# The second post-norm of a hybrid SSD / ConvFFN layer: five token tiles to ScalarE and GpSimd, three summed in PSUM, and one-column VectorE operations with scalar factors

## The chip, the cores and the metric

The kernel runs on one core of a Trainium2 chip. The core has five engines that each work through a queue of their own in order: TensorE (PE in the profile; its weight loads are PEld), VectorE (DVE), ScalarE (ACT), GpSimd (POOL) and SyncE (SP, which here issues the transfers to and from memory). SBUF is the on-chip memory of 128 partitions, PSUM the memory that TensorE's products are summed in. The metric is the device time of one execution in microseconds (us); lower is better.

## The reference, cut to what matters

One layer over 1024 latent tokens and 1024 features: a token mixer and a feed-forward network with a 3 x 3 convolution, each followed by a post-normalisation. All of it is float32. The part that the change touches is this:

```python
ALPHA = (2.0 * DEPTH) ** 0.25          # DEPTH = 1
EPS = 1e-6

def layer_norm(x):
    xf = x.astype(jnp.float32)
    mu = jnp.mean(xf, -1, keepdims=True)
    var = jnp.mean(jnp.square(xf - mu), -1, keepdims=True)
    return ((xf - mu) * lax.rsqrt(var + EPS)).astype(x.dtype)

def modulate(x, shift, scale):
    return layer_norm(x) * (1 + scale) + shift

def post_norm(x, y, gate, g, b):
    return layer_norm(ALPHA * x + gate * y) * g + b

x = post_norm(x, mix_lat, g1, ln1_g[l], ln1_b[l])                       # first post-norm
ffn_lat = conv_ffn(modulate(x, sh2, sc2), ffn_w_up[l], ffn_conv_w[l], ffn_conv_b[l], ffn_w_down[l], True)
x = post_norm(x, ffn_lat, g2, ln2_g[l], ln2_b[l])                       # second post-norm: the output
```

## The kernel before, in words

The tokens are held as eight tiles of 128 tokens (the partitions) by 1024 features, `xa[0]` to `xa[7]`. A float32 product is made of three products of parts (high by high, high by low, low by high). In the order of time the kernel has four stages that matter here.

- The mixer and its output projection (`out_tiles`), up to about 467 us.
- The first post-norm. `post1(t)` takes the statistics of a tile on VectorE (`ln_stats`, line 154), normalises it (lines 1063 and 1064), takes the statistics again for the FFN's own normalisation and applies that (`norm`); `post2` transposes two tiles on TensorE, scales them on ScalarE (line 188), rounds them on VectorE (line 193) and forms the low part on GpSimd (line 194). The tiles go from 7 down to 0, so the FFN's first products wait for tiles 1 and 0.
- The ConvFFN: for each of 44 channel tiles TensorE makes the up-projection, VectorE the convolution (line 1170, one source in PSUM, one in SBUF, one factor per partition), GpSimd the products and low parts, and TensorE the down-projection in pieces.
- The second post-norm (lines 1249 to 1323). Four channel tiles are left for the end: their products are summed in PSUM by token tile (`last_mm`, line 1266), for tiles 0 to 3 in parts ahead of time and for tiles 4 to 7 one after the other, 24 products each. `post_last(t)` then adds the sum to `xa[t]`, takes the statistics, normalises and sends the tile out.

In `post_last` the tiles are treated in two ways before the change. Tiles 1 and 3 have their statistics made by ScalarE (lines 1289 and 1294: a pass that sums and a pass that sums squares), the other six by VectorE (`bn_stats`, line 161). Tiles 0 to 3 are normalised by ScalarE (line 1299), and multiplied by `ln2_g` and shifted by `ln2_b` by GpSimd (lines 1300 and 1301, two passes of 128x1024 in SBUF); tiles 4 to 7 are normalised by VectorE in two passes (lines 1307 and 1308). The sums are added in place to `xa[t]` in SBUF, so every later VectorE pass reads SBUF alone.

The reciprocal deviation takes a handful of operations on one column, 128x1: `rstd` (line 147 and on) forms variance plus epsilon on VectorE, the square root on ScalarE (line 149), the reciprocal on VectorE (line 151), and `newton` (lines 137 to 141) a Newton step on VectorE: two products of two columns, one multiply-add with constants, one more product. `ln_stats` then forms minus the mean over the deviation (line 165). Both are also called with four or two columns earlier in the kernel; with one column only in the two post-norms.

PSUM is held as three tiles of two banks (`psa`) and two of one bank (`psb`). Tiles 2 and 6 of the second post-norm take two single banks each; the others take a pair. Tiles 5, 6 and 7 are the last users of theirs.

The kernel is written with a scheduler that orders each engine's instructions at build time by the order of the program and by its own estimate of when operands are ready, so operations of several token tiles stand interleaved in an engine's queue. That queue is then run strictly in order.

Of the kernel before, what the change touches and what calls it, by code (L numbers as in the profile page):

```python
# [26 lines left out]
def rev_ap(t, hi, n):  # L27
    """Free elements hi, hi-1, ... (n of them) of a two-dimensional tile or AP."""
    a = t[:, hi : hi + 1]
    return bass.AP(a.tensor, a.offset, [list(a.ap[0]), [-1, n]])  # L30
# [3 lines left out]
def hybrid_layer(  # L34
# [16 lines left out]
    def open_psum(na, nb):  # L51
        """PSUM as na tiles of two banks and nb of one."""
        if psx[0] is not None:
            psx[0].close()
        psx[:] = ExitStack(), na, nb
        psx.append(psx[0].enter_context(tc.tile_pool(name=f"ps{na}", bufs=1, space=PSUM, reuse_waits="tile")))
# [13 lines left out]
    # Memory that is handed from stage to stage: tags of [P, 1024] words.  # L70
# [11 lines left out]
    def half(tag, name, shape=(P, 512), dt=F32):  # L82
        """One of two tiles of 512 words of a tag of the small pool."""
# [27 lines left out]
    # columns: c 0:8, c_ctx 8:16, conv w 16:40 (tap*8+tile), conv b 40:48, norm_w 48:52, pool_scale 52:54,  # L111
    # b_ada of the first shift 54:62 and scale 62:70
# [21 lines left out]
    def newton(r, v, n, name):  # L134
        """One Newton step of r towards 1/sqrt(v)."""
        t = sm.tile([P, n], F32, tag=f"rt{n}", name=f"{name}_t")
        V.tensor_tensor(t, r, r, op=ALU.mult)
# [6 lines left out]
    def rstd(var, n, name, scale=1.0):  # L144
        """1/sqrt(var*scale + eps): square root, reciprocal, one Newton step."""
# [8 lines left out]
    def ln_stats(srcs, name):  # L154
        """Mean, 1/deviation and -mean/deviation of the rows of several token tiles, [P, tiles] each."""
# [9 lines left out]
        V.scalar_tensor_tensor(nmr, mv[:, :, 0], -1.0, r, op0=ALU.mult, op1=ALU.mult)  # L165
        return mv[:, :, 0], r, nmr

    def modulate(xns, c0, c1, sc, sh, hi, lo, tmps, lo_eng, name, via_act=False):
        """Transpose token tiles, scale and shift per feature, split into two parts; hi and lo are functions of a range
        of feature tiles."""  # L170
# [33 lines left out]
    def split(raw, hi, lo, eng=None):  # L204
        """hi = raw rounded to float32r, lo = raw - hi (exact)."""
# [3 lines left out]
    # ================= mixer =================  # L209
# [8 lines left out]
    def wblock(c0, name, tags=None):  # L218
        """128 columns of w_in in two parts."""
# [8 lines left out]
    def zload(j, q):  # L228
        """Half the rows of 264 columns: dt and z[0:248], or z[248:512]."""
# [17 lines left out]
    def load_wa(qd):  # L247
        """A quarter of the shift's and of the scale's columns."""
# [28 lines left out]
    hh = [htile("H0", "hh0"), htile("H1", "hh1")]  # L277
    hl = [htile("H2", "hl0"), htile("H3", "hl1")]
    ada1 = sl.tile([P, 2, 8, 2], F32, name="ada1")  # shift or scale, feature tile, latents or context

    def ada_quarter(qd):
        """Two feature tiles of the first shift and scale, for latents and context."""
# [35 lines left out]
    dtr = sl.tile([P, 10, 16], F32, tag="dtr", name="dtr")  # the 16: (group, direction, head of the group)  # L318
# [15 lines left out]
    def z_out(t, pt):  # L334
        """dt, and silu(z) of a token tile, kept in DRAM until the scan's outputs need it."""
# [90 lines left out]
    def proj_feat(w, pt, mids=()):  # L426
        """One 128-column block; the functions of mids are called between the feature tiles."""
# [51 lines left out]
    def dv(t, tl, d):  # L479
        """[P, 2 groups, 4 heads] of one direction."""  # L480
        return t[:, tl, :].rearrange("p (g d h) -> p g d h", g=2, d=2)[:, :, d, :]

    def decay_a(dct):
# [7 lines left out]
        # softplus(v) = max(v, 0) + log1p(exp(-|v|)); log1p(e) = 2 atanh(e / (2 + e))  # L491
# [896 lines left out]
```

## Time and profile before

| what | us |
|---|---|
| median of three executions | 1238.14 |
| lowest of them | 1237.48 |
| profiled execution, first to last instruction | 1238.0 |
| last product on TensorE begins | 1213.85 |
| last operation on VectorE ends | 1234.95 |
| busy in the profiled execution: TensorE / VectorE / GpSimd / ScalarE | 1159.4 / 988.0 / 467.0 / 375.3 |

The profiled execution's span stands 0.1 us beside the median. A row of the timeline gives the start, the duration, the engine, the line of the kernel, the operation, what is written and read, the shapes, and, in brackets, how long the engine was idle ahead of it and who ended that. A group "x2" is two instructions one behind the other. A row of busy time by stretch gives, for each stretch of the span, its length and then the busy time and instruction count of each engine, the granted TensorE clock, and the share and rate of the DMA engines. A row of the groups gives the busy time and the mean duration in nanoseconds, then the idle time ahead and its causes.

### The profile page before, as it was taken

The numbers are of one execution on the slowest core, as the hardware profiler recorded it, in microseconds if no ns is written. First come the engines' busy times: TensorE is split into PE (matmuls) and PEld (weight loads), VectorE is DVE, ScalarE is ACT, GpSimd is POOL, SyncE is SP. The second block draws the span as 40 slices with busy tenths as digits, with TensorE's granted clock in tenths as the row PEclk, the third lists the DMA queues.
The fourth block names the chain that finished last, engine by engine and source line by source line (L and its number), as shares of the span: only waits on it lengthen the run. The fifth ranks groups of instructions, "written<-read, shape, count | busy, mean of one in ns | idle before, by whom it ended". The sixth has DMA issues, their size and how long they took to land.

```text
span 1238.0 us, 14349 instructions
## 1 busy us (share of the span) xinstructions
PE 1159.4 (94%) x5463; PEld 943.4 (76%) x5463; DVE 988.0 (80%) x1426; ACT 375.3 (30%) x559; POOL 467.0 (38%) x243
## 2 busy tenths in 40 slices
PE   4999998889978998999999999999999999999992
PEld 2798877768756886788888888888888888888881
DVE  4788799999898889798777777777777777778958
ACT  2263566712344132432222212222212122222140
POOL 0010143353352033575353435353434344353254
PEclk9999998989889998999999999999999999999996
DMA  9848555556624011221110212110211112011012
GB/s 314 293 146 298 169 159 173 167 198 219 221 77 171 33 35 51 86 68 51 34 55 31 69 34 68 35 52 34 68 34 50 53 34 69 27 58 52 2 50 119
DMA packets 104637, 122.52 MB, mean 99 GB/s; under 512 B 7006, under 2 KB 83564, under 8 KB 104568
## 3 DMA queue, kind: packets, MB, share of 16 engines
q1 hardware_dynamic: 104567, 121.60, 30.3%
q8 instruction: 43, 0.70, 0.2%
q14 instruction: 27, 0.21, 0.1%
HBM read 106.82 MB, written 14.76 MB: 98 GB/s over the span
## 4 chain that ended last, share of the span: by engine, by line
PE 74%; DVE 16%; DMA 4%; issue 3%; ACT 1%; POOL 1%; SPq 0%; DVEq 0%; ACTq 0%; POOLq 0%
PE pu L1219 37%; PE pdn L1144 16%; PE pout L994 4%; PE px L433 4%; PE pz L332 4%; PE pl L1266 2%; DMA bc<-cs_scratch 1%; PE pu L1180 1%; DVE EU L631 1%; DMA wa<-in_w_ada_dram 1%; DVE pn_st L161 1%; DVE st L696 1%; PE pp L433 1%; DVE xa L1063 1%; PE pd L896 1%
## 5 line engine op out<-in xcount | busy, mean ns | idle before, releaser
L1170 DVE SCALAR_TENSOR_TENSOR cv<-pu,ffc,cv 128x945 f32<-128x945 f32 (+7 forms) x368 | 432.6, 1177 | 20.5 <-ACT cv L1162 10.7
L1219 PE MATMUL pu<-h2h,wul 128*128 128x512 f32 x656 | 205.5, 394 | 0.0
L1219 PE MATMUL pu<-h2h,wuh 128*128 128x512 f32 x656 | 205.2, 394 | 0.0
L1219 PE MATMUL pu<-h2l,wuh 128*128 128x512 f32 x656 | 204.5, 393 | 0.0
L1147 DVE TENSOR_TENSOR xa<-xa,pdn 128x512 f32<-128x512 f32 x128 | 87.4, 683 | 128.9 <-PE pdn L1144 128.6
L207 POOL TENSOR_TENSOR wul<-wur,wuh 128x1024 fp32r<-128x1024 f32 x44 | 106.0, 2409 | 207.9 <-ACT wuh L206 207.9
L1219 PEld LDWEIGHTS pu<-h2h,wuh 128*128 128x128 f32 x656 | 123.3, 188 | 28.9
L1219 PEld LDWEIGHTS pu<-h2l,wuh 128*128 128x128 f32 x656 | 123.3, 188 | 28.6
L1219 PEld LDWEIGHTS pu<-h2h,wul 128*128 128x128 f32 x656 | 123.3, 188 | 27.8
L206 ACT ACTIVATE wuh<-wur 128x1024 fp32r<-128x1024 f32 x44 | 46.3, 1054 | 237.1 <-PE pu L1219 221.5
L1144 PE MATMUL pdn<-wdh,gl 128*128 128x512 f32 x288 | 113.3, 394 | 0.0
L1144 PE MATMUL pdn<-wdl,gh 128*128 128x512 f32 x288 | 113.3, 393 | 0.0
L1144 PE MATMUL pdn<-wdh,gh 128*128 128x512 f32 x288 | 113.1, 393 | 0.0
L1242 POOL TENSOR_TENSOR wdr<-wdr,g2b 128x1024 f32<-128x1024 f32 x22 | 53.0, 2411 | 68.4 <-DMA wdr<-in_ffn_w_down_dram 68.4
L1238 POOL TENSOR_TENSOR cv<-cv,cv 128x1024 f32<-128x1024 f32 (+1 forms) x23 | 53.1, 2308 | 60.5 <-ACT cv L1237 60.4
L207 POOL TENSOR_TENSOR gl<-cv,gh 128x1024 fp32r<-128x1024 f32 (+1 forms) x23 | 53.4, 2320 | 42.3 <-ACT gh L206 42.3
L1144 PEld LDWEIGHTS pdn<-wdh,gh 128*128 128x128 f32 x288 | 54.1, 188 | 12.9
L1144 PEld LDWEIGHTS pdn<-wdh,gl 128*128 128x128 f32 x288 | 54.1, 188 | 12.4
L1144 PEld LDWEIGHTS pdn<-wdl,gh 128*128 128x128 f32 x288 | 54.1, 188 | 12.2
L1162 ACT ACTIVATE cv<-pu,ffc 128x1024 f32<-128x1024 f32 (+3 forms) x46 | 53.1, 1154 | 29.0 <-PE pu L1219 18.8
L1237 ACT ACTIVATE cv<-cv 128x1024 f32<-128x1024 f32 (+1 forms) x23 | 23.5, 1022 | 120.6 <-DVE cv L1170 120.6
L207 POOL TENSOR_TENSOR wdl<-wdr,wdh 128x1024 fp32r<-128x1024 f32 x22 | 52.8, 2414 | 4.7 <-ACT wdh L206 4.7
(348 smaller groups left out, 2142.9 us busy)
## 6 DMA issues: line engine op xcount, KB each, us to landing
wur<-in_ffn_w_up_dram SPq DMA_DIRECT2D x44, 512.0 KB
wad<-in_w_ada_dram SPq DMA_DIRECT2D x32, 512.0 KB
wdr<-in_ffn_w_down_dram SPq DMA_DIRECT2D x22, 512.0 KB
wa<-in_w_ada_dram SPq DMA_DIRECT2D x32, 256.0 KB
bc<-cs_scratch SPq DMA_DIRECT2D x32, 256.0 KB
xr<-in_x_dram SPq DMA_DIRECT2D x8, 512.0 KB
wx_r<-in_w_in_dram SPq DMA_DIRECT2D x8, 512.0 KB
m_scratch<-EU SPq DMA_DIRECT2D x16, 256.0 KB
```

Source lines behind the costliest of these rows:

```text
L206: S.activation(hi, raw, AF.Identity)
L207: (eng or G).tensor_tensor(lo, raw, hi.bitcast(F32), op=ALU.subtract)
L332: TE.matmul(pt[:, j * 512 : j * 512 + ZW], a, b[:, k % 4, :], start=first and i == 0, stop=last and i == 2)
L433: TE.matmul(pt[:, q * 512 : q * 512 + 512], a[:, k, :], b[q][:, k, :], start=k == 0 and i == 0, stop=k == KD - 1 and i == 2)
L994: TE.matmul(pt[:, nb * 512 : nb * 512 + 512], u, v[:, nb * 512 : nb * 512 + 512], start=first and i == 0, stop=last and i == 2)
L1144: TE.matmul(pt, u_, v_[:, s], start=i == 0, stop=i == n - 1)
L1147: V.tensor_tensor(xa[t][:, s], xa[t][:, s], pt, op=ALU.add)
L1162: S.activation(acc[:, a * 64 : b * 64], pt[:, a * 64 : b * 64], AF.Identity, bias=ffc[:, 396 + ct : 397 + ct], scale=ffc[:, 176 + ct : 177 ...
L1170: last = V.scalar_tensor_tensor(dst, pv[:, r0 + dy : r1 + dy, c0 + dx : c1 + dx], ffc[:, w * 44 + ct : w * 44 + ct + 1], dst, op0=ALU.mult ...
L1219: TE.matmul(pt[:, q * 512 : q * 512 + 512], a[:, k, :], b[q][:, k, :], start=k == 0 and j == 0, stop=k == KD - 1 and j == 2)
L1238: G.tensor_tensor(acc[:, s], acc[:, s], acc_v[:, s], op=ALU.mult)
L1242: G.tensor_tensor(raw, raw, g2b, op=ALU.mult)
```

## The change

Three things change; elsewhere the difference between the two files removes comments only.

1. With one column, `newton` uses three `tensor_scalar` operations in place of four operations. The factors that were second tensors are now per-partition scalars. `ln_stats` forms its third result in the same way. This holds for the sixteen calls in the first post-norm and, as far as `newton` goes, for the eight of the second.
2. In `post_last`, tiles 0 to 3 all take their statistics on ScalarE; tile 4 takes them on VectorE; tiles 0 to 4 are normalised by ScalarE and scaled and shifted by GpSimd.
3. Tiles 5, 6 and 7 have the residual added into PSUM: the sum stays there, the statistics are read from there, the first normalising pass is done in place there, and the second writes to SBUF. Tiles 6 and 7 go by halves, each half with a transfer of its own.

```diff
     def newton(r, v, n, name):
         t = sm.tile([P, n], F32, tag=f"rt{n}", name=f"{name}_t")
+        if n == 1:
+            V.tensor_scalar(t, r, r, v, op0=ALU.mult, op1=ALU.mult)
+            V.tensor_scalar(t, t, -0.5, 1.5, op0=ALU.mult, op1=ALU.add)
+            q = sm.tile([P, n], F32, tag=f"rq{n}", name=f"{name}_q")
+            V.tensor_scalar(q, t, r, None, op0=ALU.mult)
+            return q
         V.tensor_tensor(t, r, r, op=ALU.mult)
         V.tensor_tensor(t, t, v, op=ALU.mult)
...
     def ln_stats(srcs, name):
...
-        V.scalar_tensor_tensor(nmr, mv[:, :, 0], -1.0, r, op0=ALU.mult, op1=ALU.mult)
+        if n == 1:
+            V.tensor_scalar(nmr, mv[:, :, 0], r, -1.0, op0=ALU.mult, op1=ALU.mult)
+        else:
+            V.scalar_tensor_tensor(nmr, mv[:, :, 0], -1.0, r, op0=ALU.mult, op1=ALU.mult)
...
+    NPOOL = 5
+
     def post_last(t):
-        z = xa[t]
-        if accs[t][2] is not None and t < NT - 1:
-            V.tensor_tensor(z, z, accs[t][2], op=ALU.add)
+        z, pt = xa[t], accs[t][2]
+        late = t >= NPOOL
+        halves = [slice(nb * 512, nb * 512 + 512) for nb in range(2)]
+        dst = [accs[t][nb] if late else z[:, s] for nb, s in enumerate(halves)]
+        if pt is not None and t < NT - 1:
+            V.tensor_tensor(pt if late else z, z, pt, op=ALU.add)
         else:
+            for nb, s in enumerate(halves):
+                V.tensor_tensor(dst[nb], z[:, s], accs[t][nb], op=ALU.add)
+        if late or t == NPOOL - 1:
+            mv = sm.tile([P, 2], F32, tag="bmv1", name=f"pn2_{t}_mv")
+            st = sm.tile([P, 2, 6], F32, tag="bst", name=f"pn2_{t}_st")
             for nb in range(2):
-                s = slice(nb * 512, nb * 512 + 512)
-                V.tensor_tensor(z[:, s], z[:, s], accs[t][nb], op=ALU.add)
-        if t not in (1, 3):
-            mu, r, nmr = ln_stats([z], f"pn2_{t}")
+                V.bn_stats(st[:, nb, :], dst[nb])
+            V.bn_aggr(mv, st)
+            mu = mv[:, 0:1]
+            r = rstd(mv[:, 1:2], 1, f"pn2_{t}")
         else:
             sc = cvt(f"lnsc{t}")
             acc2 = sm.tile([P, 2], F32, tag="lnacc", name=f"lnacc{t}")
             S.activation(sc, z, AF.Identity, accum_out=acc2[:, 0:1])
             nmu = sm.tile([P, 1], F32, tag="nmu", name=f"nmu{t}")
-            mu = sm.tile([P, 1], F32, tag="mu", name=f"mu{t}")
             V.tensor_scalar(nmu, acc2[:, 0:1], -1.0 / D, None, op0=ALU.mult)
-            V.tensor_scalar(mu, acc2[:, 0:1], 1.0 / D, None, op0=ALU.mult)
             S.activation(sc, z, AF.Square, bias=nmu, accum_out=acc2[:, 1:2])
             r = rstd(acc2[:, 1:2], 1, f"pn2_{t}", scale=1.0 / D)
+        if not late:
             nmr = sm.tile([P, 1], F32, tag="nmr1", name=f"nmr{t}")
-            V.tensor_tensor(nmr, nmu, r, op=ALU.mult)
-        if t < 4:
+            if t == NPOOL - 1:
+                V.tensor_scalar(nmr, mu, r, -1.0, op0=ALU.mult, op1=ALU.mult)
+            else:
+                V.tensor_scalar(nmr, nmu, r, None, op0=ALU.mult)
             S.activation(z, z, AF.Identity, bias=nmr, scale=r)
             G.tensor_tensor(z, z, lng, op=ALU.mult)
             G.tensor_tensor(z, z, lnb, op=ALU.add)
             nc.sync.dma_start(out[0, t * P : (t + 1) * P, :], z)
+        elif t < NT - 1 and pt is not None:
+            V.scalar_tensor_tensor(pt, pt, mu, lng, op0=ALU.subtract, op1=ALU.mult)
+            V.scalar_tensor_tensor(z, pt, r, lnb, op0=ALU.mult, op1=ALU.add)
+            nc.sync.dma_start(out[0, t * P : (t + 1) * P, :], z)
         else:
-            n = 2 if t == NT - 1 else 1
-            for h in range(n):
-                s = slice(h * D // n, (h + 1) * D // n)
-                V.scalar_tensor_tensor(z[:, s], z[:, s], mu, lng[:, s], op0=ALU.subtract, op1=ALU.mult)
-                V.scalar_tensor_tensor(z[:, s], z[:, s], r, lnb[:, s], op0=ALU.mult, op1=ALU.add)
+            for nb, s in enumerate(halves):
+                V.scalar_tensor_tensor(dst[nb], dst[nb], mu, lng[:, s], op0=ALU.subtract, op1=ALU.mult)
+                V.scalar_tensor_tensor(z[:, s], dst[nb], r, lnb[:, s], op0=ALU.mult, op1=ALU.add)
                 nc.sync.dma_start(out[0, t * P : (t + 1) * P, s], z[:, s])
```

## The prediction

> **What bounds the kernel now.** I read the busy time by stretch first, then the timeline of the two stretches in which TensorE is not full, then the groups of the last stretch.
>
> ```profile
> span 1238.0 us, 14349 instructions
> ```
> ```profile
> core 0: us, PE busy (x) PEld busy (x) DVE busy (x) ACT busy (x) POOL busy (x), PEclk, DMA share, GB/s
> 440.00:480.00 40.00, 39.55 (x191) 32.02 (x189) 38.68 (x82) 15.19 (x28) 18.88 (x11) 1.00 0.23 66
> 480.00:498.20 18.20, 11.51 (x55) 8.90 (x55) 16.29 (x37) 6.57 (x15) 6.48 (x5) 0.81 0.00 0
> ...
> 1187.80:1214.30 26.50, 26.45 (x115) 21.11 (x113) 25.33 (x57) 11.30 (x18) 12.63 (x6) 1.00 0.10 40
> 1214.30:1238.00 23.70, 0.00 (x0) 0.00 (x0) 20.45 (x43) 0.61 (x3) 7.32 (x3) 0.56 0.34 133
> ```
> ```profile
> 700.00:900.00 200.00, 200.00 (x867) 162.61 (x866) 145.74 (x145) 44.29 (x42) 86.52 (x37) 1.00 0.16 48
> ```
>
> In the ConvFFN TensorE is busy 200 of 200 us, so whatever starts it earlier ends it earlier. It has two holes: 6.7 us (18.20 - 11.51) in the first post-norm, and the last 23.7 us, where it has nothing left and VectorE is busy for 20.45. Only these can give anything, and the change touches both. In the last stage VectorE is not slow by its work but by waits inside its instructions:
>
> ```profile
> 1198.01 2.41 POOL L1300 TENSOR_TENSOR xa<-xa,ln2g 128x1024 f32<-128x1024 f32 x1 [12.22 <-ACT xa L1299]
> ...
> 1209.86 2.40 POOL L1300 TENSOR_TENSOR xa<-xa,ln2g 128x1024 f32<-128x1024 f32 x1
> ...
> 1216.00 5.62 POOL L1301 TENSOR_TENSOR xa<-xa,ln2b 128x1024 f32<-128x1024 f32 x2
> ```
> ```profile
> 1187.87 1.22 DVE L1279 TENSOR_TENSOR xa<-xa,pl 128x1024 f32<-128x1024 f32 x1 [12.24 <-PE pl L1266]
> ...
> 1209.94 2.32 DVE L1297 TENSOR_TENSOR nmr<-nmu,pn_q 128x1 f32<-128x1 f32 x1
> ...
> 1221.25 0.14 DVE L147 TENSOR_SCALAR pn_v<-pn_mv 128x1 f32<-128x1 f32 x1
> ...
> 1227.83 0.68 DVE L1283 TENSOR_TENSOR xa<-xa,pl 128x512 f32<-128x512 f32 x1
> ...
> 1233.27 0.16 DVE L141 TENSOR_TENSOR pn_q<-pn_r,pn_t 128x1 f32<-128x1 f32 x1
> 1233.46 0.16 DVE L165 SCALAR_TENSOR_TENSOR pn_nmr<-pn_mv,pn_q 128x1 f32<-128x1 f32 x1
> 1233.54 1.41 DVE L1308 SCALAR_TENSOR_TENSOR xa<-xa,pn_q,ln2b 128x512 f32<-128x512 f32 x2
> ```
>
> At 1209.94 a product of two single columns takes 2.32 us and ends at 1212.26, with the GpSimd pass that runs beside it (1209.86 + 2.40). The same kind takes 0.16 at 1233.27, where GpSimd is done. A VectorE operation with two tensors in SBUF is held until the running GpSimd pass ends. The one-tensor operation at 1221.25 is not: 0.14 us, inside a GpSimd pass that ends at 1221.62. What the holds cost stands in the groups from 1187.8 on:
>
> ```profile
> L1308 DVE SCALAR_TENSOR_TENSOR xa<-xa,pn_q,ln2b 128x1024 f32<-128x1024 f32 (+1 forms) x5 | 7.4, 1499 | 0.0
> ...
> L137 DVE TENSOR_TENSOR pn_t<-pn_r 128x1 f32<-128x1 f32 x8 | 4.2, 537 | 0.0
> ...
> L141 DVE TENSOR_TENSOR pn_q<-pn_r,pn_t 128x1 f32<-128x1 f32 x8 | 3.3, 425 | 0.0
> L138 DVE TENSOR_TENSOR pn_t<-pn_t,pn_v 128x1 f32<-128x1 f32 x8 | 2.8, 364 | 0.0
> L165 DVE SCALAR_TENSOR_TENSOR pn_nmr<-pn_mv,pn_q 128x1 f32<-128x1 f32 x6 | 2.8, 464 | 0.1
> L1297 DVE TENSOR_TENSOR nmr<-nmu,pn_q 128x1 f32<-128x1 f32 x2 | 2.5, 1238 | 0.0
> ...
> L1299 ACT ACTIVATE xa<-xa,nmr,pn_q 128x1024 f32<-128x1024 f32 x2 | 2.5, 1237 | 6.3 <-DVE nmr L1297 6.3
> ...
> L1294 ACT ACTIVATE lnsc<-xa,nmu 128x1024 f32<-128x1024 f32 x2 | 2.3, 1138 | 0.0
> L1289 ACT ACTIVATE lnsc<-xa 128x1024 f32<-128x1024 f32 x2 | 2.1, 1062 | 9.0 <-DVE xa L1279 9.0
> ...
> L149 ACT ACT_TABLE_LOAD x1 | 1.3, 1283 | 0.0
> ```
>
> The five one-column groups take 15.6 us for 32 operations; at the unheld 0.16 us they would take 5.1. Line 1308 takes 7.4 for three whole passes and two halves; four times the 1.41 of its last row is 5.6. Holds: about 12.3 us.
>
> **The change part by part: the last stage.** Part 1 makes every one-column operation a one-tensor one. Part 3 gives every large VectorE pass one source in PSUM. That this combination, with a factor per partition, runs free beside GpSimd is shown by the convolution:
>
> ```profile
> 1172.55 2.43 POOL L207 TENSOR_TENSOR wdl<-wdr,wdh 128x1024 fp32r<-128x1024 f32 x1
> ```
> ```profile
> 1170.41 5.22 DVE L1170 SCALAR_TENSOR_TENSOR cv<-pu,ffc,cv 128x512 f32<-128x512 f32 x7
> ```
>
> Seven passes in 5.22 us, 0.75 each, through a GpSimd pass. So no VectorE operation of the new last stage should be held, and the end is the later of two chains.
>
> VectorE's chain. The last product begins at 1213.85 and takes 0.4. Tile 7's second addition begins at 1227.83 and the last pass ends at 1234.95, 7.1 us, of which 1.3 is a pass of tile 6 in between; with part of tile 6 still in the way I take 6.4: 1214.3 + 6.4 = 1220.7. From 1234.95 to the span's end it takes 3.05 us, so 1223.8. VectorE's other work hides under the products: it loses the statistics of tiles 0 and 2, tile 4's two passes and the holds, so there is no backlog at 1214.3. No row shows writing to PSUM from VectorE. Its bounds are 0.74 us a half pass (as line 1308's) and twice that; I take the first, being next to the convolution's 0.75 with a PSUM source. Twice would add some 2.6 us on tile 7's four such operations. A `tensor_scalar` with column factors lies between 0.14 (line 147) and 0.3, so at most 0.5 us on the last chain.
>
> GpSimd's chain. Ten passes instead of eight, 2.41 each: 24.1 us. Its start: the first addition ends at 1189.1; then on ScalarE the summing pass (1.06) and the squaring pass (1.14), with some 0.2 each to read out the sum, the table load and square root (some 1.5), five one-column operations at 0.19 each (from 1233.27 to 1233.46) with the hops between engines (some 0.7), and the normalisation (1.24). That is 1196.1 bare. If tile 1's two passes go in between it is 1198.7, if tile 2's go too 1201.3. I take 1198.0, where the first pass begins today and near the first two. So 1198.0 + 24.1 = 1222.1. A whole tile's transfer of 512 KB instead of 256 KB costs
>
> ```profile
> 1204.50:1205.00 0.50, 0.50 (x3) 0.40 (x3) 0.50 (x4) 0.50 (x2) 0.03 (x1) 1.00 1.00 410
> ```
>
> at 410 GB/s 0.6 us more than the 3.05 above, less what overlaps: 3.5. The end is 1225.6, behind VectorE's 1223.8. SP issues in order: if tile 4's transfer stands ahead of tile 7's, tile 7's two follow by about 1 us, inside the range. ScalarE's load (4 x 2.6 + 5 x 1.24 + 1.3 + square roots, some 20 us from 1189) runs faster than GpSimd's 4.8 a tile. **The last stage gives 1238.0 - 1225.6 = 12.4 us.**
>
> **The first post-norm.** Here VectorE sets when TensorE can go on:
>
> ```profile
> 448.73 1.07 DVE L137 TENSOR_TENSOR pn_t<-pn_r 128x1 f32<-128x1 f32 x1
> 449.83 1.21 DVE L138 TENSOR_TENSOR pn_t<-pn_t,pn_v 128x1 f32<-128x1 f32 x1
> ...
> 457.71 1.26 DVE L137 TENSOR_TENSOR ln_t<-ln_r 128x1 f32<-128x1 f32 x1
> ...
> 474.70 1.16 DVE L137 TENSOR_TENSOR ln_t<-ln_r 128x1 f32<-128x1 f32 x1
> ...
> 476.55 0.81 DVE L308 TENSOR_SCALAR xn<-xa,ln_mv,ln_q 128x1024 f32<-128x1024 f32 x1
> ...
> 489.94 1.35 DVE L308 TENSOR_SCALAR xn<-xa,ln_mv,ln_q 128x1024 f32<-128x1024 f32 x1 [0.57 <-PE h L177]
> ```
> ```profile
> 473.45 2.40 POOL L207 TENSOR_TENSOR wul<-wur,wuh 128x1024 fp32r<-128x1024 f32 x1 [4.43 <-ACT wuh L206]
> ...
> 489.45 1.29 POOL L194 TENSOR_TENSOR h2l<-h2t,h2h 128x512 fp32r<-128x512 f32 x1 [0.36 <-DVE h2h L193]
> ```
> ```profile
> 485.91 0.20 ACT L149 ACTIVATE ln_s<-ln_v 128x1 f32<-128x1 f32 x1 [4.98 <-DVE ln_v L147]
> ```
> ```profile
> 487.07 1.12 PE L177 MATMUL h<-mat,xn 128*128 128x128 f32 x4 [5.34 <-ACT h2t L188]
> ```
>
> TensorE's 5.34 us end with ScalarE's row at 485.91: a square root that stands in its queue ahead of the scaling and waits for VectorE. Four products are held there by 0.9, 1.1, 1.1 and 1.0 us, and seven calls on the way lose one operation each, 0.19 where it is dependent, less where it is interleaved: up to 1.3. Upper bound 5.4 us, under the 6.7 of the hole. Lower bound: the holds pass on whole to the next operation with two SBUF tensors, lines 1063 and 1064, which stay: 0, and a slip of the queues' order could cost a microsecond. I take 3.0, a little over half: the hold at 474.70 frees 0.7 at least, since line 308 would then wait for GpSimd until 475.85 instead of starting at 476.55. TensorE is full in the ConvFFN and VectorE is not (146 of 200 us), so the 3.0 go to the end whole.
>
> **Sum:** 1238.0 - 12.4 - 3.0 = 1222.6; the span stands 0.1 below the median, which I leave out.
>
> A rule that speaks against the change: the Trainium skill's SBUF — State Buffer, Who interferes with whom, says that `tensor_scalar` too can take the port pair that VectorE shares with GpSimd. VectorE: DVE Perf Modes, Mode 2×_2P, ties that to an outermost dimension that can be split evenly. The trace agrees for wide ones (line 308: 0.81 us free, 1.35 beside the GpSimd pass that ends at 490.74). The one-column row at 1221.25 was not held. By the rule at its widest the time would be that of the second rival.
>
> **The rivals.**
> - The first post-norm gives nothing: the holds move to lines 1063 and 1064. Then 1225.6, with 1223 to 1228 by the start of GpSimd.
> - The new one-column operations are held as the old ones were. Against it: 1221.25; for it: the rows have constants as factors, not columns. Then VectorE gets about one such operation through for each GpSimd pass and leaves the last pass, 1222.1 and some 1.5 for its turns, with the work that it now has from 1221.6 on, 13.3 us: 1236.9, and 3.05 to the end: 1240, slower than before. It decides against the change once VectorE has over 11.4 us of work left at GpSimd's end (1238.0 - 3.05 - 1223.6).
> - GpSimd, the new bound, starts late: each ScalarE pass pair queued ahead of the first normalisation adds 2.6 us. Three pairs put the start at 1203.9 and the end at 1228.5, or 1231.5 without the first post-norm's 3. It takes a start after 1213 to lose all, and nothing points there.
> - The whole hole of the first post-norm closes (6.7) and GpSimd starts at 1196.1: 1217 (1196.1 + 24.1 + 3.5 - 6.7), VectorE's chain giving the same floor (1223.8 - 6.7).
>
> **How the numbers follow.** The forecast 0.62 (1218 to 1226, its own range), no gain in the first post-norm 0.17, one-column operations held 0.07, a late GpSimd 0.08, the whole hole 0.06. The range 1217 to 1230 leaves out the held operations and half of the late starts, 0.11; its width is that of the start of GpSimd and of the first post-norm's 0 to 6.7. A measurement of this kernel tells about 2% from no change: 24.8 us. Faster than 1213.4 is under the floor of 1217 (0.02), slower than 1262.9 needs two rivals at once (0.01), within 2% is the rest (0.97).
>
> **What would show it.** Right: no one-column VectorE row over 0.3 us anywhere beside GpSimd; large passes of tiles 5 to 7 at 0.75 a half; ten GpSimd passes back to back from about 1195 on that timeline (3 earlier by the first part), the last one ending after VectorE's last; TensorE's wait at 487 shorter by 3. Wrong: one-column rows of 1 to 2.4 us; PSUM passes near 1.5 us a half; gaps between GpSimd's passes with ScalarE as the releaser; or VectorE's last row after GpSimd's.

## The result and the profile after

The changed kernel takes 1229.43 us in the median of four executions (1228.78 to 1230.26), the kernel before 1237.81 beside it: a ratio of 0.9932, with a 95% interval of 0.9918 to 0.9947. That is 8.4 us, inside the predicted range of 1217 to 1230 and inside 2%, but 6.8 us above the predicted 1222.6. One of the four executions of the kernel before took 1640.35 us; without it their median is 1237.48. The profiled execution has a span of 1227.9 us, 10.1 less than the one before.

Three rows of the timeline cut each execution into four stretches: the first up-projection product on TensorE, the first product of the ConvFFN's main loop, and the first addition of the last stage on VectorE. First those of the kernel before (its first addition, at 1187.87, is shown in the prediction), then those of the kernel after:

```profile
467.68 0.48 PE L1180 MATMUL pu<-h2h,wuh 128*128 128x512 f32 x1
...
514.50 0.62 PE L1219 MATMUL pu<-h2h,wuh 128*128 128x512 f32 x2
```
```profile
466.44 0.49 PE L1190 MATMUL pu<-h2h,wuh 128*128 128x512 f32 x1
...
511.30 0.62 PE L1229 MATMUL pu<-h2h,wuh 128*128 128x512 f32 x2
```
```profile
1185.33 1.22 DVE L1295 TENSOR_TENSOR xa<-xa,pl 128x1024 f32<-128x1024 f32 x1 [12.24 <-PE pl L1276]
```

| stretch | before | after | difference |
|---|---|---|---|
| mixer, up to the first up-projection product | 467.68 | 466.44 | -1.24 |
| first post-norm, up to the main loop's first product | 46.82 | 44.86 | -1.96 |
| ConvFFN, up to the first addition (1187.87; 1185.33) | 673.37 | 674.03 | +0.66 |
| last stage, up to the end (1238.0; 1227.9) | 50.1 | 42.6 | -7.6 |

The mixer's 1.24 us is no part of the change: in the twelve profiled executions of this study that product began between 462.2 and 469.3, in no order that goes with an edit. The other three stretches repeat closely, so the experiments below are read in them, and the medians beside them.

The last stage after, in the groups from 1185 on. Columns: what is done, busy time and mean duration in ns, idle time ahead:

```profile
L1322 POOL TENSOR_TENSOR xa<-xa,ln2g 128x1024 f32<-128x1024 f32 x5 | 11.9, 2388 | 13.0 <-ACT xa L1321 13.0
...
L1331 DVE SCALAR_TENSOR_TENSOR pl<-pl,pn_mv,ln2g 128x512 f32<-128x512 f32 x4 | 3.0, 750 | 0.0
L1332 DVE SCALAR_TENSOR_TENSOR xa<-pl,pn_q,ln2b 128x512 f32<-128x512 f32 x4 | 2.9, 744 | 0.1
...
L139 DVE TENSOR_SCALAR pn_t<-pn_r,pn_v 128x1 f32<-128x1 f32 x8 | 2.1, 267 | 0.1
L142 DVE TENSOR_SCALAR pn_q<-pn_t,pn_r 128x1 f32<-128x1 f32 x8 | 1.6, 207 | 0.0
```

In this stage nothing on VectorE is held any more: the one-column products, which had a mean of 364 to 537 ns (lines 137, 138 and 141), are now at 207 and 267, and the normalising passes at 0.74 to 0.75 a half, as lines with a PSUM source were in the convolution. GpSimd's passes run back to back. The end is in the timeline: GpSimd's first and last pass, VectorE's last pass, and SyncE's issues (SPq).

```profile
1196.28 2.42 POOL L1322 TENSOR_TENSOR xa<-xa,ln2g 128x1024 f32<-128x1024 f32 x1 [12.99 <-ACT xa L1321]
...
1218.01 2.35 POOL L1323 TENSOR_TENSOR xa<-xa,ln2b 128x1024 f32<-128x1024 f32 x1
```
```profile
1219.34 0.75 DVE L1332 SCALAR_TENSOR_TENSOR xa<-pl,pn_q,ln2b 128x512 f32<-128x512 f32 x1
```
```profile
1201.21 19.51 SPq L1324 DMA_DIRECT2D out_dram<-xa  x5
1220.81 0.38 SPq L1328 DMA_DIRECT2D out_dram<-xa  x1
1221.29 3.40 SPq L1333 DMA_DIRECT2D out_dram<-xa  x4
```

Line 1324 sends out tiles 0 to 4, lines 1328 and 1333 tiles 5 to 7. The fifth transfer of line 1324 waits for GpSimd's last pass, which ends at 1220.36 (1218.01 + 2.35), and the five transfers of tiles 5, 6 and 7 stand behind it in SyncE's queue. Tile 5 had been normalised by 1211.08 (1209.80 + 1.28), tile 6 by 1215.21 (1213.82 + 1.39):

```profile
1209.80 1.28 DVE L1327 SCALAR_TENSOR_TENSOR xa<-pl,pn_q,ln2b 128x1024 f32<-128x1024 f32 x1
...
1213.82 1.39 DVE L1332 SCALAR_TENSOR_TENSOR xa<-pl,pn_q,ln2b 128x512 f32<-128x512 f32 x2
```

The busy time by stretch (the last two columns are the DMA engines' share and rate) shows no transfer from 1220 to 1221 and then 2 MB at nearly full rate:

```profile
1220.00:1221.00 1.00, 0.00 (x0) 0.00 (x0) 0.09 (x1) 0.00 (x0) 0.36 (x1) 0.50 0.00 0
1221.00:1222.00 1.00, 0.00 (x0) 0.00 (x0) 0.00 (x0) 0.00 (x0) 0.00 (x0) 0.50 0.81 324
1222.00:1223.00 1.00, 0.00 (x0) 0.00 (x0) 0.00 (x0) 0.00 (x0) 0.00 (x0) 0.50 1.01 410
...
1226.00:1227.00 1.00, 0.00 (x0) 0.00 (x0) 0.00 (x0) 0.00 (x0) 0.00 (x0) 0.50 0.55 217
```

From the last pass to the end it is 7.5 us (1227.9 - 1220.36); before it was 3.05.

### The profile page after: what moved, and what is told of

The parts are those of the page before. It is cut to its first block, busy times and chain, and to the rows that moved or that the text cites. A ratio compares the mean times of both kernels' runs of the same rounds, so it can differ in the third digit from the quotient of the medians.

```text
span 1227.9 us, 14332 instructions
## 1 busy us (share of the span) xinstructions
PE 1158.6 (94%) x5463; PEld 940.4 (77%) x5463; DVE 968.0 (79%) x1393; ACT 380.3 (31%) x568; POOL 470.5 (38%) x245
## 4 chain that ended last, share of the span: by engine, by line
PE 72%; DVE 13%; issue 5%; DMA 4%; POOL 4%; ACT 1%; SPq 0%; POOLq 0%; DVEq 0%; ACTq 0%
PE pu L1229 37%; PE pdn L1154 16%; PE pout L1004 4%; PE pz L342 4%; PE px L443 3%; PE pu L1190 2%; DMA bc<-cs_scratch 1%; DVE EU L641 1%; POOL xa L1322 1%; DMA wa<-in_w_ada_dram 1%; POOL xa L1323 1%; PE pp L443 1%; PE pd L906 1%; DVE EU L620 1%; DVE st L706 1%
## 5 line engine op out<-in xcount | busy, mean ns | idle before, releaser
L1154 PEld LDWEIGHTS pdn<-wdh,gh 128*128 128x128 f32 x288 | 54.0, 188 | 12.4
```

Source lines behind the costliest of these rows:

```text
L1154: TE.matmul(pt, u_, v_[:, s], start=i == 0, stop=i == n - 1)
```

## The experiments

Profiled executions by stretch, as in the table above, and the times. The ratio is to the kernel before, run beside each.

| kernel | median us | ratio, interval | first post-norm | ConvFFN | last stage |
|---|---|---|---|---|---|
| before (profile above) | 1237.81 | 1 | 46.82 | 673.37 | 50.1 |
| after (profile above) | 1229.43 | 0.9932 [0.9918, 0.9947] | 44.86 | 674.03 | 42.6 |
| after, a second time | 1227.52 | 0.9921 [0.9901, 0.9941] | 43.70 | 674.03 | 42.6 |
| part 1 alone | 1230.96 | 0.9944 [0.9927, 0.9962] | 43.63 | 673.38 | 45.2 |
| all but part 1 | 1238.10 | 0.9993 [0.9979, 1.0008] | 46.72 | 674.03 | 48.6 |
| all but part 3 | 1233.05 | 0.9964 [0.9946, 0.9983] | 43.63 | 674.02 | 46.0 |
| old first post-norm | 1229.06 | 0.9940 [0.9919, 0.9960] | 46.82 | 674.03 | 42.6 |
| transfers of tiles 5 to 7 on ScalarE | 1224.85 | 0.9888 [0.9860, 0.9916] | 43.68 | 674.03 | 39.2 |
| four tiles on GpSimd | 1225.70 | 0.9896 [0.9877, 0.9914] | 44.84 | 674.03 | 38.4 |
| products ahead of the transposes | 1233.83 | 0.9961 [0.9946, 0.9976] | 46.90 | 675.64 | 42.6 |
| transfers on ScalarE, early table | 1223.25 | 0.9877 [0.9836, 0.9918] | 43.66 | 673.38 | 38.0 |
| the same, four tiles on GpSimd | 1224.04 | 0.9868 [0.9828, 0.9908] | 43.64 | 673.38 | 37.7 |

**Part 1 alone.** The kernel before with the one-column operations of the change.

```diff
+        if n == 1:
+            V.tensor_scalar(t, r, r, v, op0=ALU.mult, op1=ALU.mult)
...
-            V.tensor_tensor(nmr, nmu, r, op=ALU.mult)
+            V.tensor_scalar(nmr, nmu, r, None, op0=ALU.mult)
```

> The kernel before with part 1 of the change alone (one-column operations with scalar factors, in both post-norms); tiles, engines and PSUM as before. Theory A (a hold is taken by the next operation with two SBUF tensors): the one-column rows fall to 0.3 us or less, but lines 1063/1064 in the first post-norm and 1307/1308 in the second, which still read two SBUF tensors, become the ones that wait; the first post-norm gives 1.5 to 2 us, the last stage 1 to 5, so 1231 to 1235 against 1237.8 before. Rival B (the holds go away with the column products): the last stage gives all of the 10.5 us that the five column groups lost, 1226 or less. Rival C (tensor_scalar is held as well): 1237 to 1240.

The last stage went from 50.1 to 45.2. Its groups on VectorE:

```profile
L1316 DVE SCALAR_TENSOR_TENSOR xa<-xa,pn_mv,ln2g 128x1024 f32<-128x1024 f32 (+1 forms) x5 | 9.8, 1970 | 0.0
L1317 DVE SCALAR_TENSOR_TENSOR xa<-xa,pn_q,ln2b 128x1024 f32<-128x1024 f32 (+1 forms) x5 | 8.6, 1733 | 0.0
...
L138 DVE TENSOR_SCALAR pn_t<-pn_r,pn_v 128x1 f32<-128x1 f32 x8 | 2.0, 263 | 0.0
```

In the kernel before, the second of these two lines took 7.4 us (line 1308, in the prediction), and the first:

```profile
L1307 DVE SCALAR_TENSOR_TENSOR xa<-xa,pn_mv,ln2g 128x1024 f32<-128x1024 f32 (+1 forms) x5 | 5.4, 1085 | 0.0
```

Theory A: the one-column rows are free, 5.1 us in place of 15.6, but the two large passes, which kept two inputs in SBUF, take 18.4 us in place of 12.8, where free ones would take 11.2 (twice the prediction's 5.6). Of the 10.5 us that the small operations no longer take, 5.6 have moved to the next large ones, and 4.9 are gained.

**All but part 1.** The kernel after with the one-column operations of the kernel before (`if n == 0` in `newton` and `ln_stats`, and the old products in `post_last`).

> The kernel after without part 1: tiles, engines and PSUM as changed, but the one-column operations in their old form everywhere. Theory A (the scalar factors are what lets VectorE run beside GpSimd's ten passes, so parts 2 and 3 need part 1): every column product of the last stage is held to the end of a GpSimd pass, three for each of eight tiles; tile 7's three alone cost some 5 to 7 us, and the first post-norm loses its 2 us: 1234 to 1242. Theory B (VectorE has slack in the last stage under the transfers, so the holds there cost little): it loses only the first post-norm's 2 us and at most 1 more, 1231 to 1232.5.

Theory A: 48.6 us, so parts 2 and 3 without part 1 give 1.5, and part 1 is worth 6.0 on top of them. Not as the expectation had it, though: tile 7's own three products ran free at 0.16, after GpSimd's end. The loss lies earlier, in VectorE's chain: its last pass ends 45.7 us after the first addition in place of 34.8, and the end comes 2.9 behind it. Products of tiles 2 to 6 are held in it, two of them in these rows:

```profile
1202.78 2.26 DVE L148 TENSOR_TENSOR pn_q<-pn_r,pn_t 128x1 f32<-128x1 f32 x1
...
1219.63 2.05 DVE L144 TENSOR_TENSOR pn_t<-pn_r 128x1 f32<-128x1 f32 x1
...
1230.17 0.75 DVE L1332 SCALAR_TENSOR_TENSOR xa<-pl,pn_q,ln2b 128x512 f32<-128x512 f32 x1
```

The held products of tiles 2 and 3 also make ScalarE late with their normalisation, and so GpSimd itself, which now waits ahead of its fifth and its seventh pass and ends 3.9 us later; that is not what sets the end here:

```profile
1206.59 2.40 POOL L1322 TENSOR_TENSOR xa<-xa,ln2g 128x1024 f32<-128x1024 f32 x1 [1.57 <-ACT xa L1321]
...
1214.60 2.34 POOL L1322 TENSOR_TENSOR xa<-xa,ln2g 128x1024 f32<-128x1024 f32 x1 [3.14 <-ACT xa L1321]
```

**All but part 3.** The sums of tiles 5 to 7 go to SBUF again and both passes read SBUF alone; tile 4 stays on GpSimd.

```diff
-        dst = [accs[t][nb] if late else z[:, s] for nb, s in enumerate(halves)]
+        dst = [z[:, s] for s in halves]
...
-            V.tensor_tensor(pt if late else z, z, pt, op=ALU.add)
+            V.tensor_tensor(z, z, pt, op=ALU.add)
...
-            V.scalar_tensor_tensor(pt, pt, mu, lng, op0=ALU.subtract, op1=ALU.mult)
-            V.scalar_tensor_tensor(z, pt, r, lnb, op0=ALU.mult, op1=ALU.add)
+            V.scalar_tensor_tensor(z, z, mu, lng, op0=ALU.subtract, op1=ALU.mult)
+            V.scalar_tensor_tensor(z, z, r, lnb, op0=ALU.mult, op1=ALU.add)
```

> The changed kernel with the sums of tiles 5, 6 and 7 kept in SBUF as before (part 3 undone); parts 1 and 2 stay. Theory A (a large pass with two SBUF tensors is held by GpSimd, a pass with one tensor in PSUM is not): GpSimd is busy without a break from 1196 to 1220, so the ten pass rows of tiles 5 to 7 are held, rows of 2 to 3.5 us, GpSimd's own passes lengthen by the turns VectorE takes, and the end comes 4 to 9 us later than the changed kernel, 1233 to 1238. Rival B (only the one-column products were worth anything; the large passes fit between): within 1.5 us of the changed kernel, 1228 to 1231.

Its groups on VectorE, beside the 3.0 and 2.9 us of the kernel after, and GpSimd's multiplications, beside 11.9:

```profile
L1331 DVE SCALAR_TENSOR_TENSOR xa<-xa,pn_mv,ln2g 128x512 f32<-128x512 f32 x4 | 6.3, 1572 | 0.0
...
L1332 DVE SCALAR_TENSOR_TENSOR xa<-xa,pn_q,ln2b 128x512 f32<-128x512 f32 x4 | 4.9, 1262 | 0.0
...
L1327 DVE SCALAR_TENSOR_TENSOR xa<-xa,pn_q,ln2b 128x1024 f32<-128x1024 f32 x1 | 3.4, 3356 | 0.0
```
```profile
L1322 POOL TENSOR_TENSOR xa<-xa,ln2g 128x1024 f32<-128x1024 f32 x5 | 13.9, 2771 | 13.0 <-ACT xa L1321 13.0
```

Theory A, a little under its 4 to 9 us: the stage takes 46.0, and part 3 is worth 3.4 on top of the other two. The 3.4 came through GpSimd: without part 3 the two engines' large passes hold each other, and GpSimd's last pass ends 38.4 us after the first addition in place of 35.0, with the same 7.5 us from there to the end, since SyncE's queue waits for that pass here too. VectorE's last pass ends 41.8 after the first addition in place of 34.8, so part 3 shortened that chain by 7.0, of which the queue let 3.4 through. The queue is also why this kernel loses 0.8 against part 1 alone (45.2): VectorE's last pass ends 0.4 earlier than there (42.2), but the end is 4.2 behind it in place of 3.0.

**Transfers of tiles 5 to 7 on ScalarE.** The kernel after, with these five transfers issued from ScalarE's queue.

```diff
-            nc.sync.dma_start(out[0, t * P : (t + 1) * P, :], z)
+            nc.scalar.dma_start(out[0, t * P : (t + 1) * P, :], z)
...
-                nc.sync.dma_start(out[0, t * P : (t + 1) * P, s], z[:, s])
+                nc.scalar.dma_start(out[0, t * P : (t + 1) * P, s], z[:, s])
```

> The changed kernel with the transfers of tiles 5, 6 and 7 issued from ScalarE's queue instead of SP's. Theory A (SP's queue is in order, and tile 4's transfer, which waits for GpSimd's last pass at 1220.4, holds back the five transfers of tiles 5 to 7, 1.5 MB, so that 2 MB move after the last pass): tiles 5 and 6 leave earlier, only tile 4's and the end of tile 7's are left, and the end moves from 1227.9 to about 1224 in the profile, 3.5 to 4.5 us faster than the changed kernel: 1225 to 1226. Rival B (the end is GpSimd's last pass plus a fixed time for a transfer): within 1 us of the changed kernel, 1228.5 to 1230. Rival C (ScalarE's queue, now waiting with transfers, delays the square roots of tiles 6 and 7): 1230 or more.

The stage falls from 42.6 to 39.2. ScalarE's queue (ACTq) sends each tile out when it is done, while GpSimd's last pass still runs:

```profile
1208.78 0.37 ACTq L1328 DMA_DIRECT2D out_dram<-xa  x1
1212.25 1.00 ACTq L1333 DMA_DIRECT2D out_dram<-xa  x2
1214.01 0.20 ACT L156 ACTIVATE pn_s<-pn_v 128x1 f32<-128x1 f32 x1 [7.66 <-DVE pn_v L154]
1216.21 1.92 ACTq L1333 DMA_DIRECT2D out_dram<-xa  x2
```
```profile
1215.64 2.35 POOL L1323 TENSOR_TENSOR xa<-xa,ln2b 128x1024 f32<-128x1024 f32 x1
```

GpSimd's last pass ends at 1217.99, and the end at 1222.2 is 4.2 us later in place of 7.5. The two chains before it did not move: from the first addition it is 35.0 us to GpSimd's end and 34.8 to VectorE's, here and in the kernel after. That is theory A; rival C is out, since the square roots on ScalarE did not delay VectorE.

**Four tiles on GpSimd.** `NPOOL = 4` in place of 5: tile 4 is normalised in PSUM by VectorE, and its transfer too comes from line 1328.

> The changed kernel with four tiles on ScalarE and GpSimd instead of five (tile 4 is summed in PSUM and normalised by VectorE like tiles 5 to 7; tile 3 takes its statistics on VectorE). Theory A (GpSimd's tenth pass and the transfers queued behind it set the end): GpSimd ends 4.8 us earlier, at about 1215.6 on the profile of the changed kernel, the transfers of tiles 4 to 6 go out before VectorE's last pass, and the end is VectorE's last pass plus 3: VectorE gets some 2.5 us more to do, of which up to 2 reach its last pass (1220 to 1222): 1223 to 1225 on the profile, 3 to 5 us faster than the changed kernel, 1225 to 1227. Rival B (VectorE is the bound once it takes tile 4): its last pass moves by 2.5 to 4 us and the end with it, 1228 to 1231.

38.4 us, as theory A had it: GpSimd is done at 1215.32. Tiles 4 and 5, normalised by 1205.75 and 1210.54, wait for it in SyncE's queue behind tile 3's transfer, but they go out while VectorE finishes tile 7, and the end stands 3.6 behind VectorE's last pass (1219.81 + 0.75). That pass ends 34.8 us after the first addition, as in the kernel after, so tile 4's two passes did not reach it. The fifth tile on GpSimd, with SyncE's queue as it was, cost 4.2 us.

**The first post-norm, and the kernel after again.** Both in one series with the next experiment.

```diff
-        if n == 1:
+        if n == 1 and name.startswith("pn2"):
...
-        if n == 1:
+        if n == 0:
```

> The kernel after, with the first post-norm's one-column operations as they were before the change (the second post-norm's stay as changed). It measures the first post-norm's share alone. Theory A (the holds moved to the two large normalising passes, and a good half of TensorE's shorter wait was given back because the products right after it ran at half clock): slower than the kernel after by 1.3 to 2.2 us, 1230.7 to 1231.7; column products of 0.9 to 1.2 us again in the first post-norm, TensorE's wait there near 5.3 us, and a half-clock stretch of the same 6.5 us or so as with the shorter wait. Theory B (the predicted term of 3.0 was right and the shortfall lies in the last stage alone): slower by 3.0, 1232.4. Theory C (the first post-norm gave nothing): 1229.4.

> The kernel after, unchanged, beside the others of this series on the same chip: 1229.4, within 1 us. It is what the other runs of the series are set against.

The medians stand 1.5 apart with overlapping intervals, which settles nothing. The stretch does: 46.82 with the old operations, to the hundredth what the kernel before had, against 44.86 and 43.70 in the two profiles of the kernel after. The first post-norm's share is thus 1.96 us in one, as theory A had it, and 3.12 in the other, near theory B's 3.0; theory C is out. That the same kernel has two values is taken up at the end.

**Products ahead of the transposes.** TensorE's wait in the first post-norm (3.19 us after, 5.34 before) is at a transpose, with up-projection products ready behind it. Half of those are put ahead.

```diff
-        up_half(first[n], wu[n], 1)
-        if n == 1:
-            post2((3, 2), n32)
+        up_half(first[n], wu[n], 1, range(KD if n < 2 else 4))
+    post2((3, 2), n32)
+    up_half(first[2], wu[2], 1, range(4, KD))
```

> The kernel after, with half of the third channel tile's up-projection (twelve products, ready since 479) placed ahead of the transposes of tiles 3 and 2 in TensorE's queue and the other half behind them. Nothing else is changed. Theory A (TensorE's remaining wait in the first post-norm is an order of its queue, and the half clock follows from the idle time): no idle time over 1 us from 478 to 490 on the timeline, the granted clock stays at 1.00 there, and the gain is the 3.2 us of the wait and most of the half-clock loss of some 1.5 us: 1224.7 to 1226.2. Theory B (the clock falls at this place whatever TensorE does): idle gone, but products still at 0.43 us apart for some 6 us: about 1227. Theory C (the wait moves to the transposes of tiles 1 and 0, which wait for VectorE): a hole of 2 to 3 us near 487 to 492, and no gain over 1 us.

A miss: the median is 6.3 us above that of the kernel after in the same series. The wait is gone where it stood, shorter ones come at the next transposes, somewhat as theory C had it, and after the last of these products a third that none had:

```profile
483.67 0.66 PE L187 MATMUL h<-mat,xn 128*128 128x128 f32 x4 [1.46 <-ACT h2t L198]
485.30 1.12 PE L187 MATMUL h<-mat,xn 128*128 128x128 f32 x4 [0.98 <-ACT h2t L198]
...
509.11 1.11 PE L1229 MATMUL pu<-h2h,wuh 128*128 128x512 f32 x2 [3.91 <-DVE cv L1180]
```

The main loop needs the PSUM of the first channel tile, which VectorE's convolution gives back only then; its first step on ScalarE had come at 501.58, behind a rounding that waited for GpSimd. So the first post-norm took 46.90 us, and 1.6 more went in the ConvFFN. That wait is not TensorE's alone to close. The clock did not stay at 1.00 either, as theory A had wanted (rows at the end).

**Two further versions.** Both kernels move the transfers to ScalarE and load the square root's table while ScalarE is idle; the second also has `NPOOL = 4`.

```diff
+    warm = sm.tile([P, 1], F32, tag="warm", name="warm")
+    S.activation(warm, group[-1][1][:, T - 1 : T].bitcast(F32), AF.Sqrt, scale=0.0)
```

> The kernel after with two edits: the transfers of tiles 5 to 7 are issued by ScalarE, and a square root of one column is put behind ScalarE's last rounding of the last channel tile, so that the square root's table is loaded while ScalarE is idle. From the first addition of the last stage to the end, the kernel after takes 42.6 us and with the transfers alone moved 39.2. Theory A (in that second kernel VectorE's chain, 34.8 us from the first addition to its last pass, and GpSimd's, 35.0, end together, so that only the later of them counts): GpSimd starts and ends 1.3 us earlier, VectorE's last pass does not move, and the stage gives at most 0.3 more: 38.9 to 39.2 us. Theory B (GpSimd alone sets the end): the whole 1.3 us comes through, 37.9 us. The time lies between 1220 and 1226, by where the mixer ends.

> The same two edits with four tiles on GpSimd in place of five. GpSimd's chain loses two passes (4.8 us) and the two square roots' wait; VectorE takes tile 4's two passes from PSUM (2.6 us). Theory A (VectorE now sets the end alone, and its last pass stands 34.8 us behind the first addition whatever GpSimd does): the stage takes 38.2 to 38.6 us, as with four tiles and all transfers on SyncE (38.4), so the queue no longer matters. Theory B (tile 4's passes fall into VectorE's last chain): 40 to 41 us. Theory C (the early table also shortens VectorE's backlog): 37.5.

38.0 and 37.7 us. With five tiles GpSimd ends 33.7 us after the first addition (1.3 earlier, as theory A had it) and VectorE's last pass 34.6 after it, so VectorE sets the end; but the gain was theory B's, since the way from the later of the two to the end fell from 4.2 to 3.4, tile 4's transfer no longer coming last (SyncE had issued it by 1216.30, ScalarE the last of tile 7 by 1217.30). With four tiles VectorE's last pass did not move (34.8), and the result lies between theories A and C: ScalarE's queue still saved 0.7 against four tiles on SyncE, all of it behind VectorE's last pass. With the queue out of the way the fifth tile on GpSimd makes next to no difference (38.0 with it, 37.7 without); no run shows a gain from it. By the ratios both are 1.2% to 1.3% faster than before. Against the kernel after the intervals of the ratios touch or overlap, so that they beat it rests on the last stage, 4.6 and 4.8 us shorter.

## Why the prediction was right, and where it was not

**The sign and the range** held, and the mechanisms that carry the sum were there; their sizes were off. The point was 6.8 us too low. In the profiled execution 5.3 of them are found: the last stage gave 4.84 less than predicted, the first post-norm 1.04 less, the ConvFFN took 0.66 more, and the mixer, by chance, 1.24 less. The other 1.5 are the step from that span to the median time. The prediction set the span of the kernel before beside a median of other executions and found 0.1 between them; in the kernel after, one and the same execution has a span of 1227.9 and a time of 1229.71. Set against the prediction's own terms:

**The last stage: 12.4 predicted, 7.6 measured.** The prediction's 1225.6 is 37.73 us after the first addition; it took 42.57. GpSimd's start was 0.82 later (10.95 us after the first addition, 10.13 taken), its ten passes took 24.08 (24.1 taken), and the way from there to the end 7.54 (3.5 taken). 0.82 - 0.02 + 4.04 is the 4.84 that is missing.

**The step that failed** is the sentence on SyncE: "if tile 4's transfer stands ahead of tile 7's, tile 7's two follow by about 1 us, inside the range". The order was foreseen as a possibility, but it was priced at tile 7's two transfers alone and left out of the sum. Not only those but all five of tiles 5 to 7 stood behind, 1.5 MB that had been ready or nearly so; with tile 4's that is 2 MB, which at the 410 GB/s quoted for that step are some 5.1 us. With the 2.4 that are left of the 3.05 before when its last 256 KB are taken off (0.64), an estimate from these rows is 7.5, as measured. Moving those five to another queue gave 3.4 us back, and having no such wait (four tiles) 4.2. The Trainium skill (DMA: Bandwidth & Descriptors, Issuing engines are not separate DMA queues) says that issuing from several engines only saves the time that a sequencer takes to initiate a transfer. The measured 3.4 us are of another kind: the DMA engines stood idle from 1220 to 1221 and were then busy at 0.81 to 1.01 up to 1226, so it was not the issuing that cost, but the queue's wait for GpSimd with finished transfers behind it.

**No held operation** was right, and so was the rate of passes in PSUM: in the two post-norms no one-column row beside GpSimd over 0.27 us, and in the last stage 0.74 to 0.75 a half pass, at the lower of the two bounds. The rule of the Trainium skill that was weighed there (SBUF — State Buffer, Who interferes with whom) did not apply to one column. That parts 1 and 3 were each needed is shown by the runs without them: 6.0 and 3.4 us. Part 2's fifth tile was not needed: with four tiles the last stage is shorter (38.4 us against 42.6, and 37.7 against 38.0).

**VectorE's chain** was mis-sized without effect in the kernel after. Its last pass was to end 6.4 us after the products; it ended at 1220.09 (1219.34 + 0.75), 8.4 us after the last product's end (1211.31 + 0.40):

```profile
1211.31 0.40 PE L1276 MATMUL pl<-wdh,gl 128*128 128x512 f32 x1
...
1211.74 0.70 DVE L1298 TENSOR_TENSOR pl<-xa,pl 128x512 f32<-128x512 f32 x1 [0.48 <-PE pl L1276]
...
1212.47 0.69 DVE L1298 TENSOR_TENSOR pl<-xa,pl 128x512 f32<-128x512 f32 x1
```

The 6.4 were counted from tile 7's second addition, as the 7.1 before were, less a part of tile 6. But the first addition waits for the last product too and comes ahead of it (0.73 from start to start), and tile 6 stood in the way whole: from the second addition to the end of the last pass it took 7.62. So GpSimd, which the prediction had ending 1.4 us after VectorE, ended only 0.27 after it (1220.36): that GpSimd came last, as forecast, was near to luck. The chain shows once GpSimd is out of the way: in the kernels with four tiles it sets the end.

**The first post-norm: 3.0 predicted, 1.96 measured**, and 3.1 to 3.2 in six of the eight profiled executions that have this first post-norm and nothing else moved in it; in the other two 1.96 and 1.98. The mechanism was as described, but little of the holds moved: line 1073 has three held passes (2.21, 2.08 and 2.48 us where a free one takes 1.28), as its counterpart, line 1063, had before (2.23, 2.33 and 2.57), and only one held pass of line 1074 is new (2.20). TensorE's wait fell by 2.15, from 5.34 to 3.19, not by the 3 that the prediction gave as its sign. The 3.0 was a choice between bounds of 0 and 5.4, so that six executions come within 0.2 of it is in part luck; what parts the other two from them is a matter that the prediction did not have, TensorE's clock (below).

**"The 3.0 go to the end whole"** was nearly right: the ConvFFN took 0.66 us more in the kernel after. It takes 673.37 or 673.38 in the kernel before, with part 1 alone and in the two further versions, and 674.02 or 674.03 in the others but one (675.64, products ahead). So the step goes with the kernel and is not jitter; what makes it was not found, and the count of products is the same.

**The rivals.** No gain in the first post-norm, held one-column operations and a GpSimd late by whole pairs of passes are each ruled out by rows above; the whole hole closed in no run.

## What to carry to other kernels

When work moves from one engine to another, its transfer moves in the issuing queue too: list that queue in order, and for each entry that waits add up the bytes that are ready behind it. When an engine that holds another through a shared resource gets more work, free all of the other's operations, small and large; freeing only one kind moves the holds to the next. And where run-to-run jitter elsewhere is as large as the effect, compare stretches between two rows of the trace rather than spans.

## What the runs showed of the hardware

**The half clock comes in whole windows.** A stretch at half clock began during each long wait of TensorE in the first post-norm. Busy time by stretch; the granted clock is the third column from the end, and a value between 0.50 and 1.00 gives the moment of the step. The kernel before, after, and after with the transfers moved:

```profile
483.00:484.00 1.00, 0.00 (x0) 0.00 (x0) 1.00 (x1) 0.00 (x0) 0.00 (x0) 0.70 0.00 0
...
490.00:491.00 1.00, 1.00 (x5) 0.76 (x5) 1.00 (x1) 0.98 (x3) 0.74 (x1) 0.89 0.00 0
```
```profile
481.00:482.00 1.00, 0.00 (x0) 0.00 (x0) 0.60 (x4) 0.51 (x2) 0.00 (x0) 0.93 0.00 0
...
488.00:489.00 1.00, 1.00 (x5) 0.77 (x4) 1.00 (x3) 0.00 (x0) 0.64 (x2) 0.66 0.00 0
```
```profile
480.00:481.00 1.00, 0.00 (x0) 0.00 (x0) 0.60 (x4) 0.66 (x3) 0.00 (x0) 0.93 0.00 0
...
484.00:485.00 1.00, 1.00 (x6) 0.87 (x5) 0.63 (x1) 1.00 (x3) 1.00 (x1) 0.86 0.00 0
```

Before, the clock is halved from 483.40 (0.70 means 0.60 us at half) to 490.22, 6.8 us; after, from 481.86 to 488.68, 6.8 us again, though the wait was 2.2 us shorter; in the third, with the same wait of 3.18, from 480.86 to 484.28, 3.4 us. So it lasts one window of 3.4 us or two. The Trainium skill (TensorE: Matmul & The Clock Gate, What's actually happening) gives a window of 3413 ns that runs freely beside the kernel; the trace agrees. The Trainium skill's advice on that page (Why this matters for your kernels) to keep idle gaps under some 3 us fits the waits of 3.16 to 3.31, which all cost a window here. It is not enough, though. In the kernel with products ahead, the two waits of 1.46 and 0.98 us cost a window as well, from 485.30 to 488.72:

```profile
485.00:486.00 1.00, 0.70 (x4) 0.70 (x4) 0.79 (x2) 0.25 (x1) 0.84 (x1) 0.65 0.00 0
...
488.00:489.00 1.00, 1.00 (x5) 0.71 (x5) 0.44 (x2) 1.00 (x3) 0.00 (x0) 0.64 0.00 0
```

In the 3.41 us ahead of this step TensorE was busy for 0.97 us, and in those ahead of the step in the other eleven profiled executions for 0.76 to 1.36. So the idle time of a whole window, 2.1 to 2.7 us in one piece or in two, fits all twelve, where the length of a single gap does not.

The stretch with the wait, and the row of the transposes that end it, in the kernel after:

```profile
480.00:498.20 18.20, 14.61 (x61) 11.67 (x62) 14.71 (x30) 7.97 (x16) 7.73 (x6) 0.81 0.00 1
```
```profile
482.66 1.12 PE L187 MATMUL h<-mat,xn 128*128 128x128 f32 x4 [3.19 <-ACT h2t L198]
```

This goes with the two values of one kernel. In the two executions with two windows TensorE was still idle for the first 0.76 and 0.80 us of the first one at half clock (in the kernel after, 481.86 to 482.66); in the six with one window, for 0.64 to 0.69. These eight are all that speaks for a limit between 0.69 and 0.76; no run set the moment on purpose. The same kernel after had 0.80 in one execution and 0.66 in another, so where the windows fall is chance. In the kernel after, TensorE's idle time in the stretch from 480 to 498.2 fell by 3.1 us (18.20 - 11.51 against 18.20 - 14.61), but products ran at half clock for 6.02 us (482.66 to 488.68) and before for 3.15 (487.07 to 490.22): 1.4 us of lost work more. 3.1 - 1.4 is 1.7, near the 1.96 measured.

**Factors from columns have a price of their own.** A one-column `tensor_scalar` takes 0.15 us with constants (line 140), 0.21 with one column as a factor (line 142) and 0.27 with two (line 139), beside GpSimd and alone. The old product of two columns took 0.16 where it was free, so the new forms cost a little more per operation and win by not being held.
